# Splitting attention weights during the first MLP: one piece per call against four steps of a period each

## The chip, the core and the metric

The kernel runs on one core of one Trainium2 chip. The metric is the device time of one execution in microseconds (us); a profile of one execution is read beside it. Engines are named as in the profile: PE does the matrix products, PEld loads their weights, DVE, ACT and POOL do elementwise work, and SP issues the DMA transfers. PEclk is the clock granted to PE as a share of full speed.

## The reference, cut to what matters

One sequence of 512 tokens with 1024 channels passes a pooling mixer, an MLP, a stick-breaking attention and another MLP, all in f32.

```python
def sq_relu_mlp(h, w_up, w_down):          # 1024 -> 4096 -> 1024
    u = jnp.matmul(h, w_up)
    return jnp.matmul(jnp.square(jax.nn.relu(u)), w_down)

for layer in range(DEPTH):                 # DEPTH = 2
    h = rms_norm(x, mix_pre_g[layer])
    if layer < N_A:
        m = pool_mixer(h, pool_w[layer], pool_scale[layer])
    else:
        q = jnp.matmul(h, w_q[j])...       # 16 heads of 64
        o = stick_breaking_attention(q, k, v)
        m = jnp.matmul(o..., w_o[j])
    x = x + rms_norm(m, mix_post_g[layer])
    h = rms_norm(x, mlp_pre_g[layer])
    x = x + rms_norm(sq_relu_mlp(h, w_up[layer], w_down[layer]), mlp_post_g[layer])
    if layer == N_A - 1:
        kv = jnp.matmul(rms_norm(x, kv_norm_g), w_kv)...
```

## The kernel before

*Split numbers.* PE multiplies in a type with fewer digits than f32 (fp32r in the profile). So each f32 operand is split into hi (a cast, on ACT) and lo (operand minus hi, on DVE), and a product is three matmuls (`mm3`): hi by hi, hi by lo, lo by hi. `split` does this for activations and MLP operands (lines 233 and 234), `weight` for a weight matrix: load (L117), scaling by a gain on POOL where it has one (L139, in two halves), cast (L127), subtraction (L129).

*MLP.* Each MLP has 32 up blocks (`up_block`, 24 matmuls, lines 599 to 601) followed by relu and square on ACT. The down product is taken group by group: the class `Seven` multiplies 2 x 2 blocks with seven products in place of eight (`product`, L499), for groups of 2, 3, 3, 3 and 3 blocks, 35 products in all. `left` and `right` make the operands a and w of a product by sums and differences (POOL L454, DVE L473) and a split. A group's down weights come in two halves (L438): the first into the tile w1, the second into xn3 (shown as `xn`). The last four up blocks go with four plain down matrices ("dn"), which `contract` multiplies at the end of the MLP (lines 254 to 256); these matrices take over tiles that the groups no longer need.

*Attention weights ahead of time.* The attention needs 8 v, 8 q and 8 k matrices, scaled by gains, and 8 o matrices; each is 128 x 1024, 512 KB. While the first MLP runs, `split_apart` is called after each of its products (twice after two of them). A call takes the next matrix (a piece) off the list `apart`, loads it (L181), scales it if it has a gain, casts it (L184) and subtracts (L185), in this one call; two calls later a call stores both halves to DRAM (`kept`, L171). Pieces alternate between two sets of tiles: apart0 with apart1, and the work tiles spare with grow. In the attention, `make` loads the halves back with two transfers (L193) into a weight tile.

*Tiles.* Up weights, and in the attention its weights, take the next of four tiles with the tag "w" in the pool wts (`place`). What a tile holds next is loaded when its last reader is done.

*Order.* The program names what each engine does; a scheduler that simulates the engines sets the order of instructions on each engine, except inside `manual_schedule`, where PE keeps the order of the program. Each engine then runs in that order and waits where an operand or a tile is late.

## Time and profile before

| | us |
|---|---|
| median of 3 runs | 1009.63 |
| lowest and highest | 1008.39, 1012.03 |
| profiled execution, its own time | 1010.19 |
| span of the profiled execution | 1008.4 |

| engine | busy us | share of the span |
|---|---|---|
| PE | 957.0 | 95% |
| PEld | 812.1 | 81% |
| DVE | 744.5 | 74% |
| ACT | 521.7 | 52% |
| POOL | 248.6 | 25% |

The granted clock was 0.977 of full speed in the mean. Times in the rows are counted from the start of the span. A row of the waits says which engine and line waited for which engine and line, how long in all, how many times, and the longest. A row of a timeline gives the start and the length, and in brackets the idle time just ahead of it with what ended it.

### The profile page before, as it was taken

Reading aid. Unit: us, or ns where it says so; the run is one execution under the profiler, and the core shown is the slowest. Engines: PE = TensorE matmul, PEld = TensorE weight load, DVE = VectorE, ACT = ScalarE, POOL = GpSimd, SP = SyncE. Lnnn points to the kernel's source line nnn. Section 1 sums busy time; section 2 is a strip of 40 time slices with the busy share of each in tenths; the row PEclk is TensorE's granted clock in tenths of the full one; section 3 lists DMA queues with packets and bytes.
Section 4 is the critical chain, followed back from the end, with each engine's and each line's share of the span. In section 5 each row is a group of like instructions: output and inputs, shape, how many; then the busy total and the mean of one; then the engine's idle time right before and its main releaser. Section 6 shows DMA issues by size and latency. Waiting matters only on the chain.

```text
span 1008.4 us, 12461 instructions
## 1 busy us (share of the span) xinstructions
PE 957.0 (95%) x4823; PEld 812.1 (81%) x4823; DVE 744.5 (74%) x771; ACT 521.7 (52%) x837; POOL 248.6 (25%) x166
## 2 busy tenths in 40 slices
PE   7899889899799999899999999989999999999996
PEld 6897667678588788799888899879888888888885
DVE  5988598698797883747647778886488685967856
ACT  5656555445455452655565555566554444444532
POOL 1656262283350210500000000242031120402103
PEclk9999989989899999999999999999999999999998
DMA  7277957958869632042542425233333315133002
GB/s 264 72 286 269 317 204 280 317 196 279 305 233 338 242 126 84 21 165 88 175 158 85 167 94 190 93 131 121 126 104 125 125 42 174 35 127 125 5 38 85
DMA packets 44844, 161.59 MB, mean 160 GB/s; under 512 B 4592, under 2 KB 4976, under 8 KB 44784
## 3 DMA queue, kind: packets, MB, share of 16 engines
q1 hardware_dynamic: 44784, 160.79, 45.3%
q8 instruction: 38, 0.62, 0.2%
q14 instruction: 22, 0.18, 0.1%
HBM read 125.12 MB, written 35.65 MB: 159 GB/s over the span
## 4 chain that ended last, share of the span: by engine, by line
PE 61%; DVE 14%; DMA 12%; POOL 5%; issue 4%; ACT 3%; SPq 0%; POOLq 0%; DVEq 0%; ACTq 0%
PE ps L499 17%; PE ps L599 10%; PE ps L601 10%; PE ps L600 10%; DMA kept<-apart 5%; PE ps L254 3%; PE ps L255 3%; PE ps L256 3%; PE ps L843 2%; DVE x L285 2%; PE ps L833 2%; POOL apart L139 2%; DVE w L129 2%; DMA apart<-in_wk 2%; DMA kept<-spare 1%
## 5 line engine op out<-in xcount | busy, mean ns | idle before, releaser
L499 PE MATMUL ps<-w,a 128*128 128x512 f32 x1176 | 287.7, 398 | 24.0 <-DVE w L234 12.1
L499 PEld LDWEIGHTS ps<-w,a 128*128 128x128 f32 x1176 | 224.9, 192 | 76.1 <-DVE w L234 14.7
L600 PE MATMUL ps<-xnl,w 128*128 128x512 f32 (+1 forms) x712 | 262.4, 369 | 1.1 <-DVE xnl L234 1.1
L601 PE MATMUL ps<-xnh,w 128*128 128x512 f32 (+1 forms) x712 | 262.2, 369 | 0.0
L599 PE MATMUL ps<-xnh,w 128*128 128x512 f32 (+1 forms) x712 | 261.4, 370 | 0.0
L600 PEld LDWEIGHTS ps<-xnl,w 128*128 128x128 f32 x712 | 134.8, 189 | 23.3 <-DVE xnl L234 1.3
L601 PEld LDWEIGHTS ps<-xnh,w 128*128 128x128 f32 x712 | 134.8, 189 | 22.5
L599 PEld LDWEIGHTS ps<-xnh,w 128*128 128x128 f32 x712 | 134.2, 189 | 22.1
L508 DVE TENSOR_TENSOR y<-ps,y 128x512 f32<-128x512 f32 x124 | 83.5, 683 | 45.9 <-PE ps L499 45.9
L129 DVE TENSOR_TENSOR w<-raw,w 128x1024 fp32r<-128x1024 f32 x62 | 83.8, 1355 | 36.7 <-ACT w L127 36.6
L279 POOL TENSOR_TENSOR y<-y,grow 128x512 f32<-128x512 f32 x12 | 17.9, 1493 | 319.6 <-ACT xn L237 319.6
L454 POOL TENSOR_TENSOR s<-r 128x768 f32<-128x768 f32 (+1 forms) x10 | 23.1, 2310 | 240.9 <-ACT r L530 240.9
L233 ACT CAST a<-r 128x768 fp32r<-128x768 f32 (+1 forms) x60 | 47.5, 793 | 59.0 <-PE ps L499 25.4
L233 ACT CAST w<-e 128x1536 fp32r<-128x1536 f32 (+1 forms) x30 | 41.9, 1395 | 57.8 <-DVE e L473 51.8
L127 ACT CAST w<-raw 128x1024 fp32r<-128x1024 f32 x66 | 68.7, 1042 | 3.4 <-DMA raw<-in_wup 3.0
L234 DVE TENSOR_TENSOR a<-r,a 128x768 fp32r<-128x768 f32 (+1 forms) x60 | 67.0, 1118 | 4.1 <-ACT a L233 4.0
L529 ACT ACTIVATE r<-ps 128x512 f32<-128x512 f32 x56 | 33.2, 593 | 67.4 <-PE ps L601 67.3
L454 POOL TENSOR_TENSOR r<-r 128x768 f32<-128x768 f32 (+1 forms) x20 | 53.1, 2653 | 45.0 <-DVE a L234 44.3
L234 DVE TENSOR_TENSOR w<-e,w 128x1536 fp32r<-128x1536 f32 (+1 forms) x30 | 55.8, 1860 | 4.0 <-ACT w L233 3.7
L815 DVE TENSOR_TENSOR_SCAN e<-u,begin 128x1280 f32<-128x1280 f32 x16 | 45.1, 2820 | 13.2 <-ACT u L809 13.0
L139 POOL TENSOR_TENSOR spare<-spare,gc 128x512 f32<-128x512 f32 x24 | 36.3, 1531 | 66.0 <-DMA spare<-in_wq 37.4
L139 POOL TENSOR_TENSOR apart<-apart,gc 128x512 f32<-128x512 f32 x24 | 39.2, 1652 | 33.2 <-DMA apart<-in_wk 20.5
(134 smaller groups left out, 1595.6 us busy)
## 6 DMA issues: line engine op xcount, KB each, us to landing
raw<-in_wup SPq DMA_DIRECT2D x64, 512.0 KB, 4.0
w<-kept SPq DMA_DIRECT2D x62, 512.0 KB, 4.1
kept<-apart SPq DMA_DIRECT2D x48, 512.0 KB, 4.2
w<-in_wdn SPq DMA_DIRECT2D x8, 1536.0 KB, 7.9
xn<-in_wdn SPq DMA_DIRECT2D x8, 1536.0 KB, 7.1
kept<-spare SPq DMA_DIRECT2D x16, 512.0 KB, 5.4
spare<-in_wq SPq DMA_DIRECT2D x8, 512.0 KB, 4.1
apart<-in_wk SPq DMA_DIRECT2D x8, 512.0 KB, 4.8
```

What stands on the lines that cost most here:

```text
L127: nc.scalar.copy(hi, raw)
L129: on.tensor_tensor(out=lo, in0=raw, in1=hi.bitcast(F32), op=ALU.subtract)
L139: nc.gpsimd.tensor_tensor(out=v[:, h], in0=v[:, h], in1=g[:, h].broadcast_to((P, n // 2, D // n)), op=ALU.mult)
L233: latest["act"] = nc.scalar.copy(hi, src)
L234: latest["dve"] = nc.vector.tensor_tensor(out=lo, in0=src, in1=hi.bitcast(F32), op=ALU.subtract)
L454: sub = lambda out, x, y, op=ALU.subtract: nc.gpsimd.tensor_tensor(out=out, in0=x, in1=y, op=op)
L499: nc.tensor.matmul(bank, a[:, x, q, TS[t]], w[:, z, q], start=start and q == 0 and k == 0, stop=q == self.n - 1 and k == 2, skip_group_che ...
L508: nc.vector.tensor_tensor(out=part, in0=bank, in1=part, op=ALU.add)
L599: nc.tensor.matmul(pu[:, cols], wh[:, k, :], xnh[:, k, cols], start=k == 0, stop=False)
L600: nc.tensor.matmul(pu[:, cols], wh[:, k, :], xnl[:, k, cols], start=False, stop=False)
L601: nc.tensor.matmul(pu[:, cols], wl[:, k, :], xnh[:, k, cols], start=False, stop=k == KC - 1)
L815: nc.vector.tensor_tensor_scan(out=e[:, ::-1], data0=u[:, 1:][:, ::-1], data1=begin[:, ::-1], initial=0.0, op0=ALU.mult, op1=ALU.max,)
```

## The change

`split_apart` now moves each piece by one step per call: load in the first call, scaling in the next, cast and subtraction in the third, store in the fourth. There is one call after each product. Raw pieces rotate over four tiles (grow, spare and two tiles "apart"). The hi halves alternate between the two halves of one tile "wx". This tile is taken from the up weights: the tag "w" has three tiles now, and in the attention every fourth weight goes to "wx". Only v, q and k go this way (24 pieces); the o matrices are split in the attention by `weight`. Of the four plain down matrices of an MLP, the third now takes the two tiles "apart" and the fourth a tile "w". `contract` of the MLP is put under `manual_schedule` for PE.

```diff
--- before.py
+++ after.py
@@ -156,34 +156,42 @@
         elif k == ("o", 7):
             return [att_pool[0].tile([P, NSEG], F32R, tag="w", bufs=2, name=name(x))[:, :D] for x in "hl"]
         else:
-            both = wts.tile([P, 2, D], F32R, tag="w", bufs=4, name=name("w"))
+            count[0] += 1
+            fourth = count[0] % 4 == 0 and att_pool[0] is not None
+            both = wts.tile([P, 2, D], F32R, tag="wx" if fourth else "w", bufs=1 if fourth else 3, name=name("w"))
         return [both[:, 0], both[:, 1]]
     apart, kept, going = [], {}, []
     def split_apart(mp):
-        if len(going) > 1 or not apart and going:
-            k, parts = going.pop(0)
+        if going and going[0] is not None and going[0][1] == 3:
+            k, _, raw, hi, _ = going.pop(0)
             kept[k] = dram.tile([2, P, D], F32, tag=f"kept{len(kept)}", name=name("kept"))
-            for n in range(2):
-                nc.sync.dma_start(kept[k][n], parts[n].bitcast(F32))
-        if not apart:
-            return
-        k, src, scaled = apart.pop(0)
-        if len(apart) % 2:
-            raw = mp.tile([P, D], F32, tag="apart0", name=name("apart"))
-            hi = mp.tile([P, D], F32R, tag="apart1", name=name("apart"))
-        else:
-            raw = spare_tile()
-            hi = work.tile([P, D], F32R, tag="grow", name=name("apart"))
-        nc.sync.dma_start(raw, src)
-        if scaled is not None:
-            scaled(raw)
-        nc.scalar.copy(hi, raw)
-        nc.vector.tensor_tensor(out=raw, in0=raw, in1=hi.bitcast(F32), op=ALU.subtract)
-        going.append((k, (hi, raw)))
+            for n, t in enumerate((hi.bitcast(F32), raw)):
+                nc.sync.dma_start(kept[k][n], t)
+        if apart:
+            k, src, scaled = apart.pop(0)
+            n = len(apart) % 4
+            if n < 2:
+                raw = mp.tile([P, D], F32, tag="apart", bufs=2, name=name("apart"))
+            else:
+                raw = spare_tile() if n == 2 else work.tile([P, D], F32, tag="grow", name=name("apart"))
+            nc.sync.dma_start(raw, src)
+            going.append([k, 0, raw, None, scaled])
+        for x in going:
+            k, n, raw, hi, scaled = x
+            if n == 1:
+                scaled(raw)
+            elif n == 2:
+                hi = x[3] = apart_hi[0][:, len(kept) % 2]
+                nc.scalar.copy(hi, raw)
+                nc.vector.tensor_tensor(out=raw, in0=raw, in1=hi.bitcast(F32), op=ALU.subtract)
+            x[1] += 1
+    count, apart_hi = [0], [None]
     def make():
         k, src, scaled = queue.pop(0)
@@ -220,7 +228,7 @@
                 elif what == "O" and 0 in part or what == "E":
                     for c in range(2 * i, 2 * i + (2 if what == "O" else 4)):
                         want(("o", c), wo[c])
-            apart.extend(queue[n:])
+            apart.extend(x for x in queue[n:] if x[0][0] != "o")
             queue[n - GRP : n + GRP] = queue[n : n + GRP] + queue[n - GRP : n]
         for j in range(NJ):
@@ -541,6 +549,8 @@
         groups[0].load(0)
         groups[0].squares()
+        if l == 0:
+            apart_hi[0] = wts.tile([P, 2, D], F32R, tag="wx", name=name("wx"))
         need(0, 1)
         n0 = 2 * GROUPS[0]
         first = [(ps(), get(("up", l, j))) for j in range(n0)]
@@ -564,8 +574,7 @@
             for i in range(7):
                 group.product(i, y, written if g == 0 else None)
                 if l == 0:
-                    for _ in range(2 if i == 3 and g in (1, 2) else 1):
-                        split_apart(mp)
+                    split_apart(mp)
                 if i + 2 < 7:
                     if ups:
                         up(ups.pop(0))
@@ -581,16 +590,16 @@
                         coming.make(i + 2 - 7)
                     elif i == 5:
                         piece = lambda tag, k, bufs=1: mp.tile([P, k, D], F32R, tag=tag, bufs=bufs, name=name("dn"))
-                        w, e, x, z = piece("w1", 3), piece("e", 1), piece("w", 3, 2), piece("w", 3, 2)
-                        dn_pool[0] = [
-                            [w[:, 0], w[:, 1]], [w[:, 2], e[:, 0]], [x[:, 0], x[:, 1]], [x[:, 2], z[:, 0]],
-                        ]
+                        w, e, x = piece("w1", 3), piece("e", 1), piece("w", 3, 2)
+                        c, d = (piece("apart", 1, 2)[:, 0] for _ in range(2))
+                        dn_pool[0] = [[w[:, 0], w[:, 1]], [w[:, 2], e[:, 0]], [c, d], [x[:, 0], x[:, 1]]]
         assert not apart and not going
         gpost = gain_row((R_MLP_POST0, R_MLP_POST1)[l])
         w = [get(("dn", l, j)) for j in range(plain, NJ)]
         dn_pool[0] = None
         fill(ahead)
-        contract(squares[1:], w, y, False, lambda t, y: update(t, y, gpost))
+        with tc.manual_schedule(engines={mybir.EngineType.PE}):
+            contract(squares[1:], w, y, False, lambda t, y: update(t, y, gpost))
     def up_block(pu, w, cols):
         wh = w[0].rearrange("p (k c) -> p k c", k=KC)
```

Line numbers move by up to 9: casts of pieces stand at L190, splits of operands at L241, up blocks at L608 to L610.

First place: ACT in the first MLP, at the operands of the second group's first product (a of 128x768). Pieces are `apart` and `spare`. Before:

```order
L233 CAST a_1115<-r_497 128x512
L233 CAST w_1118<-xn_80 128x1024
L184 CAST apart_1174<-apart_1173 128x1024
L184 CAST apart_1358<-spare_1357 128x1024
L529 ACTIVATE r_774<-ps_1083 128x512
L127 CAST w_1110<-raw_1111 128x1024
L530 ACTIVATE r_774<-r_774 128x512
L233 CAST a_1149<-r_774 128x768
L233 CAST w_1153<-w_995 128x1536
```

Now:

```order
L241 CAST a_1102<-r_497 128x512
L241 CAST w_1105<-xn_80 128x1024
L127 CAST w_972<-raw_973 128x1024
L190 CAST wx_498<-apart_1410 128x1024
L537 ACTIVATE r_775<-ps_1070 128x512
L538 ACTIVATE r_775<-r_775 128x512
L127 CAST w_1036<-raw_1037 128x1024
L241 CAST a_1135<-r_775 128x768
L241 CAST w_1139<-w_984 128x1536
```

Two casts of pieces stood between the operand cast into w and the next relu (L529); now there is one, behind the cast of an up matrix, and it reads a piece loaded two calls earlier.

Second place: POOL at the end of the mixer, where the norm of the last tokens is made (`stat_440` and `m_439`). Before:

```order
L250 TENSOR_TENSOR stat_356<-stat_356,mhalf 128x1
L250 TENSOR_TENSOR stat_440<-stat_440,mhalf 128x1
L294 TENSOR_TENSOR m_439<-x_73,spare_129 128x512
L250 TENSOR_TENSOR stat_440<-stat_440,mhalf 128x1
L139 TENSOR_TENSOR spare_885<-spare_885,gc 128x512 x2
L139 TENSOR_TENSOR apart_823<-apart_823,gc 128x512 x2
```

Now:

```order
L258 TENSOR_TENSOR stat_356<-stat_356,mhalf 128x1
L258 TENSOR_TENSOR stat_440<-stat_440,mhalf 128x1
L139 TENSOR_TENSOR apart_824<-apart_824,gc 128x512
L302 TENSOR_TENSOR m_439<-x_73,spare_129 128x512
L139 TENSOR_TENSOR apart_824<-apart_824,gc 128x512
L258 TENSOR_TENSOR stat_440<-stat_440,mhalf 128x1
L139 TENSOR_TENSOR spare_881<-spare_881,gc 128x512 x2
```

The first piece's scaling (L139) followed the norm; now its halves stand ahead of `m_439` and ahead of the last power.

Third place: PE at the start of the attention, at the end of the k block of the first head pair (into `ps_3245` before, `ps_3162` now) and the beginning of its q block (`ps_3360`, `ps_3277`). w_2785 and w_2701 are k's weights, w_2849 and w_2762 are q's, w_2651 and w_2578 v's. Before:

```order
L256 MATMUL ps_3284<-w_2721,xnl 128x256
L599 MATMUL ps_3245<-xnh,w_2785 128x256
L599 MATMUL ps_3360<-xnh,w_2849 128x512
L254 MATMUL ps_3394<-w_2651,xnh 128x256
L255 MATMUL ps_3394<-w_2651,xnh 128x256
L600 MATMUL ps_3245<-xnl,w_2785 128x256
L601 MATMUL ps_3245<-xnh,w_2785 128x256
L599 MATMUL ps_3245<-xnh,w_2785 128x256
```

Now:

```order
L610 MATMUL ps_3162<-xnh,w_2701 128x256
L608 MATMUL ps_3162<-xnh,w_2701 128x256
L609 MATMUL ps_3162<-xnl,w_2701 128x256
L610 MATMUL ps_3162<-xnh,w_2701 128x256
L608 MATMUL ps_3277<-xnh,w_2762 128x512
L609 MATMUL ps_3277<-xnl,w_2762 128x512
L262 MATMUL ps_3311<-w_2578,xnh 128x256
L263 MATMUL ps_3311<-w_2578,xnh 128x256
```

The k and q blocks began together, from two tiles "w". Now q's block begins right after k's last matmul, and w_2762 is given the tile that w_2701 had. On SP its load stands behind those of the plain down weights and of k:

```order
L201 DMA w_2578<-kept_1000 128x1024 x2
L201 DMA w_2640<-kept_1061 128x1024 x2
L117 DMA raw_2854<-in_wdn 128x1024
L117 DMA raw_2858<-in_wdn 128x1024
L201 DMA w_2701<-kept_1125 128x1024 x2
L117 DMA raw_3878<-in_wo 128x1024
L117 DMA raw_3916<-in_wo 128x1024
L107 DMA grow_3069<-in_grow 128x1024
L201 DMA w_2762<-kept_1156 128x1024 x2
L201 DMA w_3274<-kept_1198 128x1024 x2
L201 DMA w_3382<-kept_1337 128x1024 x2
```

In SP's order of the first MLP, from the second piece's load (`spare_881`) to the load of the second weight half of the third group, stand 19 loads of pieces, 36 stores of halves, 14 up matrices (0.524 MB each) and 8.4 MB of down weights, 44.6 MB together; to that of the second group it is 25.7 MB.

## The prediction

> **What bounds the kernel now.** I cut the span into stages first, because the share of busy time is a mean over all of them. Columns: stretch, its length, busy time and count for PE, weight load, DVE, ACT and POOL, then granted clock, DMA share and GB/s.
>
> ```profile
> core 0: us, PE busy (x) PEld busy (x) DVE busy (x) ACT busy (x) POOL busy (x), PEclk, DMA share, GB/s
> 0.00:53.72 53.72, 43.49 (x315) 39.65 (x316) 41.70 (x78) 32.70 (x73) 22.59 (x24) 0.94 0.48 165
> 53.72:74.48 20.76, 20.76 (x152) 19.81 (x153) 16.53 (x17) 12.91 (x18) 10.02 (x7) 1.00 0.86 325
> 74.48:396.08 321.60, 297.62 (x1257) 241.49 (x1255) 258.06 (x208) 163.94 (x194) 119.83 (x63) 0.95 0.70 248
> ...
> 415.00:671.00 256.00, 254.47 (x1521) 226.36 (x1522) 179.48 (x225) 147.33 (x325) 26.53 (x37) 0.99 0.37 130
> ...
> 696.98:981.45 284.47, 284.47 (x1256) 235.63 (x1256) 202.16 (x176) 136.24 (x163) 51.04 (x20) 1.00 0.29 95
> 981.45:1008.41 26.96, 17.60 (x89) 14.86 (x88) 18.01 (x30) 5.69 (x18) 9.15 (x8) 0.89 0.22 79
> ```
>
> The two MLPs run the same matmuls (1257 and 1256 of them). The second takes 284.47 us and PE never stops; the first takes 321.60, which is 37.1 more. Of this 321.60 - 297.62 = 24.0 is idle PE, and 297.62 - 284.47 = 13.15 is the slower clock (0.95). So each idle microsecond costs another 13.15 / 24.0 = 0.55, and I multiply PE stalls by 1.55. Only the first MLP prepares attention weights. The waits of PE from 50 to 420 us (total, times, longest) say what it waits for:
>
> ```profile
> PE ps L499 <- DVE w L234: 12.1, 4, 5.3
> PE ps L499 <- ACT w L233: 9.4, 2, 7.6
> PE ps L326 <- ACT xn L317: 3.9, 1, 3.9
> PE ps L499 <- DVE a L234: 2.4, 3, 1.0
> ```
>
> 12.1 + 9.4 + 2.4 = 23.9, which is the idle time of the stage: it is the MLP's own operands that come late, though the products are equally large in the second MLP. I followed the longest, 7.6 us before 129.67, back through the timelines of four engines (start, length, idle before and its releaser in brackets):
>
> ```profile
> 116.24 0.39 PE L601 MATMUL ps<-xnh,w 128*128 128x512 f32 x1
> 116.47 5.60 PE L499 MATMUL ps<-w,a 128*128 128x512 f32 x24
> 129.67 1.22 PE L499 MATMUL ps<-w,a 128*128 128x512 f32 x2 [7.60 <-ACT w L233]
> ...
> 120.06 1.05 ACT L184 CAST apart<-apart 128x1024 fp32r<-128x1024 f32 x1 [4.48 <-POOL apart L139]
> 124.52 1.04 ACT L184 CAST apart<-spare 128x1024 fp32r<-128x1024 f32 x1 [3.41 <-POOL spare L139]
> ...
> 128.15 1.47 ACT L233 CAST w<-w 128x1536 fp32r<-128x1536 f32 x1
> ...
> 117.04 2.98 POOL L139 TENSOR_TENSOR apart<-apart,gc 128x512 f32<-128x512 f32 x2 [9.39 <-DVE a L234]
> 122.45 2.04 POOL L139 TENSOR_TENSOR spare<-spare,gc 128x512 f32<-128x512 f32 x2 [2.42 <-DVE apart L185]
> ...
> 118.25 0.33 SPq L181 DMA_DIRECT2D spare<-in_wq  x1
> ```
>
> Read it backwards. PE waits for ACT's w of 128.15. ACT had stood 4.48 and 3.41 us at the casts of two attention pieces (L184), which wait for POOL to scale them (L139), and POOL started the second only when its load, issued at 118.25, was there. ACT runs in order, so relu, squares and operand casts queue up behind a piece whose data is under way. It is the rule, not one accident:
>
> ```profile
> ACT apart L184 <- POOL spare L139: 40.0, 10, 6.9
> ACT apart L184 <- POOL apart L139: 35.5, 12, 6.1
> ```
>
> 75 us of waiting in 22 casts. Most is absorbed by slack on PE's side; 24 us is not.
>
> **The change, part by part.**
>
> *Four steps a period apart: -37.1, and what stays.* A piece is loaded in one period and scaled, cast and subtracted, and stored in the next three. A period is 284.47 / 35 products = 8.1 us. In the order of ACT around that place, two casts of pieces stood back to back ahead of the relu; now one stands there, and SP issues the load about two pieces ahead. ACT's 4 us waits then have 8 to 16 us of cover, and no row of the first MLP has another cause of comparable size. Ends: all of 37.1 goes, or none. I take all, and charge separately what can come instead. The three waits for a (2.4 us in the list above) are the MLP's own order: 2.4 x 1.55 = 3.7 stays (0 to 3.7).
>
> *The stream.* Loads that go out early need bytes early. In SP's order, from the second piece's load up to the third group's second weight half, stand 44.6 MB (19 piece loads, 36 half stores and 14 up matrices of 0.524 MB each, 8.4 MB of down weights), and 25.7 MB up to the second group's. What rate does the chip give?
>
> ```profile
> 696.98:813.98 117.00, 117.00 (x517) 96.91 (x517) 83.71 (x72) 59.64 (x75) 25.69 (x11) 1.00 0.34 114
> 50.00:190.00 140.00, 128.75 (x623) 107.69 (x622) 111.29 (x95) 78.82 (x104) 63.71 (x37) 0.96 0.77 274
> 114.00:131.00 17.00, 9.40 (x39) 7.51 (x38) 10.76 (x13) 8.70 (x12) 8.34 (x6) 0.83 0.95 355
> ```
>
> The first MLP moved 274 GB/s over 140 us, 355 in the stretch where SP had a backlog (DMA share 0.95), and 325 in the stage from 53.72 to 74.48 above. The first row gives the due time: from the first product to the third group's second, which is the first to need that half, PE takes 117.0 us (517 matmuls of 0.226). The same way the second group's half is due after 246 matmuls, 55.7 us. If the first product starts at 74.48 + 5 = 79.5 (the 5 is worked out below), combining and splitting the half want 4 us, and the stretch of loads begins at 54.3 with the end of the mixer, then 44.6 MB have 79.5 + 117.0 - 4 - 54.3 = 138.2 us, which is 323 GB/s, and 25.7 MB have 76.9 us, 334 GB/s. At 355 both are in time. At 325 the first is 79.1 - 76.9 = 2.2 late and the second not later. At 274 the second is 44.6 MB in 162.7 us, 24.5 late. In before's 274, SP stood waiting for tiles, so it is what was asked for, not what was to be had; I take 325, the row of the same mix just ahead: 2.2 x 1.55 = 3.4 (0 to 38).
>
> *Fewer slots for up weights: 0.* Three tiles instead of four: a slot comes round every 3 x 8.1 = 24.4 us, its matmuls take 24 x 0.226 = 5.4, so 19 stay for cast and subtraction, 1.04 + 1.36 = 2.4 by these groups (busy, mean ns):
>
> ```profile
> L127 ACT CAST w<-raw 128x1024 fp32r<-128x1024 f32 x66 | 68.7, 1042 | 3.4 <-DMA raw<-in_wup 3.0
> L129 DVE TENSOR_TENSOR w<-raw,w 128x1024 fp32r<-128x1024 f32 x62 | 83.8, 1355 | 36.7 <-ACT w L127 36.6
> ```
>
> If the 19 were gone it would be 2.4 at each of 28 blocks; nothing suggests that.
>
> *The start: +5.* POOL's order puts the first piece's scaling, in two halves, into the last tokens' norm, one ahead of its m and one ahead of its last pow.
>
> ```profile
> 52.39 0.55 POOL L250 TENSOR_TENSOR stat<-stat,mhalf 128x1 f32<-128x1 f32 x1 [0.82 <-DVE stat L243]
> 55.79 2.04 POOL L139 TENSOR_TENSOR spare<-spare,gc 128x512 f32<-128x512 f32 x2 [2.86 <-DMA spare<-in_wv]
> ...
> 54.98 0.28 PE L599 MATMUL ps<-xnh,w 128*128 128x256 f32 x1
> 55.10 0.28 PE L600 MATMUL ps<-xnl,w 128*128 128x256 f32 x1
> ```
>
> Both halves take 2.04, and every norm step behind them feeds PE's transposes. The same piece made POOL wait 2.86 for its load here. Ends: 0 (the halves fit in POOL's gaps) to 2.04 + 2.86 = 4.9; I take 2.04, since the load goes out earlier now. The fourth up block's first half used to fill PE there; its slot is now the first block's, which is in use: 24 matmuls at 0.12 (54.98 to 55.10) = 2.9 come out of the cover (0 to 2.9). Together 5 (0 to 8).
>
> *Attention: q0, +6.4, and o, +1.* q0's tile now is k0's. So SP can load it only after k0's last matmul, and PE's next two rows are q0's. The time from issue to landing of such a load is known:
>
> ```profile
> L193 SPq DMA_DIRECT2D w<-kept x62: 319/392/543, 346.9 to 625.6; - x62
> ...
> DMA to landing us min/median/max: 3.1/4.1/8.0
> ```
>
> Behind that load SP has the next v and k pieces (w_3274, w_3382), and behind q0's first matmul PE has the v products of w_2578, which is long there and could have run. PE stands 4.1 (median; 3.1 to 8.0) and, with the clock, 4.1 x 1.55 = 6.4 (4.8 to 12.4; with only a shorter wait, because PE's rows run ahead of it, 3.1). The Trainium skill, "TensorE: Matmul & The Clock Gate", Part 1, "What's actually happening", says that the clock falls to half after about 3.4 us idle and comes back after about 3.4 us of work. By that rule this wait would add 1.7 us in place of 2.3, and the sum would be 0.6 lower. The trace speaks for more rather than less: after the wait of 3.88 us here (timeline of PE, then its stretch)
>
> ```profile
> 201.07 2.50 PE L499 MATMUL ps<-w,a 128*128 128x512 f32 x5 [3.88 <-DVE w L234]
> ...
> 195.00:208.00 13.00, 9.12 (x28) 6.94 (x27) 12.10 (x11) 5.45 (x6) 5.88 (x3) 0.74 0.67 234
> ```
>
> 28 matmuls took 9.12 us, where 28 x 0.226 = 6.3 would do (117.00 / 517 from the row of the second MLP above). So 2.8 were lost behind one wait of 3.88, more than the mean of 0.55 per microsecond gives (2.1); I keep the mean. The eight o pieces are split in attention again: 8 x 1.04 on ACT, 8 x 1.36 = 10.8 on DVE, which is busy for 179.48 of 256.00 there. Ends 0 and 8 x 2.40 = 19.2; I take 1, for the 76 us of slack.
>
> *Last down weights and the fixed order: -2 and -1.5.* The fourth plain matrix no longer needs the last product's tiles, so its split is ready earlier and the first token tile's sums end first, in both MLPs.
>
> ```profile
> 414.89 1.73 PE L326 MATMUL ps<-ident,xn 128*128 128x128 f32 x8 [3.92 <-ACT xn L317]
> ...
> 998.77 0.28 PE L256 MATMUL ps<-dn,sq 128*128 128x256 f32 x1
> ...
> 999.79 1.40 DVE L285 SCALAR_TENSOR_TENSOR x<-y,stat,x 128x512 f32<-128x512 f32 x2
> 1001.12 0.41 DVE L361 TENSOR_TENSOR y<-ps,y 128x256 f32<-128x256 f32 x1
> ```
>
> The handoff wait is 3.92 in the first (0 to -3.9; I take half). At the end, the last sums leave PE at 998.77 + 0.28 and DVE fetches them at 1001.12, behind the updates of x at 999.79: 2.07 between (0 to -2.07), of which I take 1.5, as one update of two is passed.
>
> Sum: -37.1 + 3.7 + 3.4 + 5 + 6.4 + 1 - 2 - 1.5 = -21.1. The profiled execution took 1010.19 us (span 1008.4): 989.1. Its time is 0.56 above the median of the three runs (1009.63), so 988.5 for the median.
>
> **Rivals.**
>
> *The stream stays at 274 GB/s: slower.* For it: before shows it over 140 us, with stores of the same size among the loads. Against: SP waited for tiles while it did, and 355 was granted when it had work. Place: the second half of the second and third groups' down weights, PE waiting for DVE's or ACT's w behind the load. Price 24.5 x 1.55 = 38 instead of 3.4: 988.5 + 34.6 = 1023. It decides where the lateness is (21.1 + 3.4) / 1.55 = 15.8 us, at 44.6 MB in 138.2 + 15.8 us = 290 GB/s; at less the change loses.
>
> *The wait moves to the two halves of the new hi tile.* The cast of a piece needs the store of the piece two before it to have landed. If SP is behind by more than two periods, ACT stands at the cast as now. For: SP's queue is in order, and stores stand behind loads that wait for tiles. Against: 16 us of cover. At half the old idle time: 12 x 1.55 = 18.6 in place of 3.7: 1003. This gives faster, by little.
>
> *Everything fits.* The start costs nothing, the stream 355: 988.5 - 5 - 7.1 = 976.
>
> *The change doesn't do what it says.* Then ACT's order would be as it was; the rows show otherwise. What is left is that gains and prices meet: within 3 us of before.
>
> **How the numbers follow.** About 0.3%, 3 us, is what a measurement of this kernel can tell from no change. Forecast, 982 to 996: 0.48 (stream of 311 to 345 GB/s). Everything fits, below 982: 0.15. The half gain, 996 to 1006.6: 0.17. Within 3 us: 0.08. Slower: 0.12, the slow stream. So faster 0.48 + 0.15 + 0.17 = 0.80. The range 974 to 1010 leaves out some 0.03 below and 0.15 above.
>
> **What would show it.** Right: the first MLP's stage at about 292 us with PE's waits for w under 6 us; ACT's waits for POOL at casts of pieces from 75 us to under 15; DMA above 310 GB/s in the first half of the stage; one PE wait of about 4 us for a DMA at q0. Wrong: PE waits for w released by transfers of down weights, ACT waiting for the hi tile's stores, or more than 8 us between the last mixer matmuls and the first product.

## The result, and the profile after

The changed kernel takes 999.92 us (median of 4, 998.85 to 1002.42) against 1010.83 (4 runs) for the kernel before on the same chip: ratio 0.9895, 95% interval 0.9862 to 0.9928. It is 1.05% faster where 2.1% was forecast; 988.5 us was predicted. The profiled execution took 1002.42 us, 2.5 above the median, so the stages below give a little less gain than the medians.

The stages of the changed kernel (columns as ahead of the prediction), from the last transposes of the mixer on:

```profile
55.96:78.90 22.94, 22.70 (x153) 21.27 (x153) 17.89 (x16) 13.17 (x18) 11.20 (x7) 0.93 1.00 378
78.90:382.44 303.54, 291.59 (x1256) 237.96 (x1255) 252.75 (x201) 158.81 (x187) 125.43 (x60) 0.98 0.59 216
382.44:401.91 19.47, 19.47 (x96) 16.31 (x96) 14.84 (x26) 13.67 (x34) 9.23 (x10) 1.00 0.00 1
401.91:691.66 289.75, 277.44 (x1665) 245.68 (x1664) 200.16 (x245) 164.61 (x345) 24.43 (x37) 0.99 0.32 110
691.66:993.89 302.23, 302.23 (x1345) 250.66 (x1343) 217.88 (x199) 141.47 (x179) 55.33 (x27) 1.00 0.29 95
993.89:1000.60 6.71, 0.00 (x0) 0.00 (x0) 2.98 (x8) 0.63 (x4) 0.88 (x2) 0.66 0.34 121
```

Cut at the same marks (first product, last product, last plain matmul, first product of the second MLP, last matmul), the two profiled executions compare as follows, with the prediction's terms beside:

| stage, us | before | after | change | forecast |
|---|---|---|---|---|
| start to the first product | 74.48 | 78.90 | +4.4 | +5 |
| products of the first MLP | 321.76 | 303.54 | -18.2 | -30.0 |
| plain down matrices, first MLP | 24.23 | 19.47 | -4.8 | -2 |
| attention | 276.35 | 289.75 | +13.4 | +7.4 |
| second MLP | 302.23 | 302.23 | 0 | 0 |
| tail | 9.35 | 6.71 | -2.6 | -1.5 |
| span | 1008.40 | 1000.60 | -7.8 | -21.1 |

Two rows carry the miss: the products (11.8 us less gain than forecast) and the attention (6.0 more loss). The miss would be larger without the plain matrices and the tail, which gave 3.9 more than forecast. PE's longest waits in the products and the attention (total, times, longest):

```profile
PE ps L507 <- ACT w L241: 5.4, 2, 3.7
PE ps L608 <- DMA w<-kept: 3.4, 1, 3.4
PE ps L507 <- DVE w L242: 3.1, 2, 2.7
PE ps L507 <- DVE a L242: 2.5, 2, 1.5
```

And ACT's waits at the casts of pieces, from 55 to 405 us:

```profile
ACT wx L190 <- POOL apart L139: 27.4, 12, 5.4
ACT wx L190 <- POOL spare L139: 8.2, 5, 2.9
```

The long stall of 7.6 us is gone, and ACT's waits at pieces fell from 75.5 to 35.6 us. But 12 us of idle PE are left in the products, in seven stalls from 89 to 222 us. The longest, 3.69 us before 142.11, is followed back here over PE, ACT, DVE and POOL:

```profile
142.11 0.73 PE L507 MATMUL ps<-w,a 128*128 128x512 f32 x2 [3.69 <-ACT w L241]
...
140.58 1.47 ACT L241 CAST w<-e 128x1536 fp32r<-128x1536 f32 x1 [4.78 <-DVE e L481]
...
130.15 2.59 DVE L242 TENSOR_TENSOR w<-w,w 128x1536 fp32r<-128x1536 f32 x1
132.66 2.86 DVE L191 TENSOR_TENSOR apart<-apart,wx 128x1024 f32<-128x1024 f32 x1
135.44 2.60 DVE L242 TENSOR_TENSOR a<-r,a 128x768 fp32r<-128x768 f32 x1
137.96 2.59 DVE L481 TENSOR_TENSOR e<-xn,w 128x1536 f32<-128x1536 f32 x1
...
127.38 3.74 POOL L139 TENSOR_TENSOR apart<-apart,gc 128x512 f32<-128x512 f32 x2
131.09 3.35 POOL L462 TENSOR_TENSOR r<-r 128x768 f32<-128x768 f32 x1
134.52 2.70 POOL L462 TENSOR_TENSOR r<-s,r 128x768 f32<-128x768 f32 x1
137.18 4.27 POOL L139 TENSOR_TENSOR apart<-apart,gc 128x512 f32<-128x512 f32 x2
```

ACT's w waits for DVE's e, and DVE has no gap ahead of it: it works from 130 to 140 us without a pause. What is odd is the lengths. A subtraction of 128x1024 (L191) takes 2.86 us, one of 128x768 (L242) 2.60; the kernel before shows 1.22 for 128x1024 in the second MLP (below). POOL is busy throughout, and its scaling of two halves takes 3.74 and 4.27 where 2.04 was shown. So this stall isn't a piece that is late: instructions of both engines take longer here. Split in half, the stage says where:

```profile
78.90:225.00 146.10, 134.15 (x568) 107.81 (x567) 135.93 (x99) 82.59 (x102) 102.48 (x51) 0.98 0.81 303
225.00:382.44 157.44, 157.44 (x689) 130.14 (x689) 116.83 (x104) 76.21 (x86) 22.95 (x10) 0.99 0.39 137
```

All stalls lie in the first half, with DVE 93% and POOL 70% busy. The second half has none.

The two halves also hold a control. DVE's subtraction of an up matrix (L129) reads two work tiles, which the kernel has in SBUF. Its addition into y (L516) reads one of these and one tile `ps`, which the kernel has in PSUM and PE fills with its sums. The groups in the first half (busy us, mean ns of one, idle before), then in the second:

```profile
L129 DVE TENSOR_TENSOR w<-raw,w 128x1024 fp32r<-128x1024 f32 x15 | 26.8, 1788 | 3.1 <-ACT w L127 2.9
L516 DVE TENSOR_TENSOR y<-ps,y 128x512 f32<-128x512 f32 x24 | 16.0, 678 | 0.3 <-PE ps L507 0.3
```

```profile
L129 DVE TENSOR_TENSOR w<-raw,w 128x1024 fp32r<-128x1024 f32 x12 | 14.6, 1218 | 12.5 <-ACT w L127 12.5
L516 DVE TENSOR_TENSOR y<-ps,y 128x512 f32<-128x512 f32 x38 | 25.9, 685 | 17.7 <-PE ps L507 17.7
```

The subtraction takes 1788 ns in the half with a busy POOL and 1218 in the other; the addition takes the same in both. Taken one by one in this run from 50 us on, the 53 subtractions of this line that no POOL instruction overlaps took 1.20 to 1.23 us, and the 13 that POOL overlaps for over nine tenths 1.94 in the mean.

Of the signs that the prediction named for being right, only the wait at q0 came. The products are 303.5 us and not 292, PE's waits for w 8.5 and not under 6, ACT's waits at pieces 35.6 and not under 15, and the first half of the stage moved 303 GB/s and not over 310.

### The profile page after: what moved, and what is told of

It is laid out like the page before. It is cut to its first block, busy times and chain, and to the rows that moved or that the text cites. A ratio compares the mean times of both kernels' runs of the same rounds, so it can differ in the third digit from the quotient of the medians.

```text
span 1000.6 us, 12426 instructions
## 1 busy us (share of the span) xinstructions
PE 957.6 (96%) x4823; PEld 811.4 (81%) x4823; DVE 745.1 (74%) x771; ACT 525.0 (52%) x837; POOL 249.9 (25%) x166
## 4 chain that ended last, share of the span: by engine, by line
PE 74%; DVE 11%; issue 5%; DMA 3%; ACT 3%; POOL 3%; SPq 0%; POOLq 0%; DVEq 0%; ACTq 0%
PE ps L507 22%; PE ps L609 12%; PE ps L608 12%; PE ps L610 12%; PE ps L262 4%; PE ps L263 4%; PE ps L264 4%; DVE w L242 2%; PE ps L852 2%; DVE apart L191 1%; DVE a L242 1%; PE ps L842 1%; DVE w L129 1%; POOL apart L139 1%; DMA apart<-in_wk 1%
## 5 line engine op out<-in xcount | busy, mean ns | idle before, releaser
L507 PE MATMUL ps<-w,a 128*128 128x512 f32 x1176 | 282.1, 393 | 12.0 <-ACT w L241 5.4
L507 PEld LDWEIGHTS ps<-w,a 128*128 128x128 f32 x1176 | 222.0, 190 | 61.9 <-ACT w L241 6.2
L608 PE MATMUL ps<-xnh,w 128*128 128x512 f32 (+1 forms) x712 | 262.5, 371 | 3.7 <-DMA w<-kept 3.4
L610 PE MATMUL ps<-xnh,w 128*128 128x512 f32 (+1 forms) x712 | 262.1, 369 | 0.0
L608 PEld LDWEIGHTS ps<-xnh,w 128*128 128x128 f32 x712 | 134.9, 190 | 26.2 <-issue 3.6
L610 PEld LDWEIGHTS ps<-xnh,w 128*128 128x128 f32 x712 | 135.0, 190 | 22.3
L129 DVE TENSOR_TENSOR w<-raw,w 128x1024 fp32r<-128x1024 f32 x69 | 95.1, 1379 | 51.0 <-ACT w L127 50.8
L516 DVE TENSOR_TENSOR y<-ps,y 128x512 f32<-128x512 f32 x124 | 83.9, 684 | 49.8 <-PE ps L507 49.7
L127 ACT CAST w<-raw 128x1024 fp32r<-128x1024 f32 x73 | 76.3, 1046 | 50.3 <-PE ps L610 29.7
L241 ACT CAST a<-r 128x768 fp32r<-128x768 f32 (+1 forms) x60 | 47.7, 795 | 80.1 <-PE ps L507 40.6
L139 POOL TENSOR_TENSOR apart<-apart,gc 128x512 f32<-128x512 f32 x36 | 66.2, 1861 | 24.1 <-DMA apart<-in_wk 21.2
L242 DVE TENSOR_TENSOR w<-e,w 128x1536 fp32r<-128x1536 f32 (+1 forms) x30 | 68.5, 2284 | 4.9 <-ACT w L241 4.4
L242 DVE TENSOR_TENSOR a<-r,a 128x768 fp32r<-128x768 f32 (+1 forms) x60 | 66.9, 1117 | 4.5 <-ACT a L241 4.5
L241 ACT CAST w<-e 128x1536 fp32r<-128x1536 f32 (+1 forms) x30 | 41.9, 1397 | 53.1 <-DVE e L481 43.3
L462 POOL TENSOR_TENSOR r<-r 128x768 f32<-128x768 f32 (+1 forms) x20 | 44.9, 2246 | 41.4 <-DVE a L242 40.9
L242 DVE TENSOR_TENSOR w<-w,w 128x1536 fp32r<-128x1536 f32 (+1 forms) x20 | 34.6, 1729 | 4.2 <-ACT w L241 4.2
```

What stands on the lines that cost most here:

```text
L127: nc.scalar.copy(hi, raw)
L129: on.tensor_tensor(out=lo, in0=raw, in1=hi.bitcast(F32), op=ALU.subtract)
L139: nc.gpsimd.tensor_tensor(out=v[:, h], in0=v[:, h], in1=g[:, h].broadcast_to((P, n // 2, D // n)), op=ALU.mult)
L241: latest["act"] = nc.scalar.copy(hi, src)
L242: latest["dve"] = nc.vector.tensor_tensor(out=lo, in0=src, in1=hi.bitcast(F32), op=ALU.subtract)
L462: sub = lambda out, x, y, op=ALU.subtract: nc.gpsimd.tensor_tensor(out=out, in0=x, in1=y, op=op)
```

## The experiments

Times are medians; ratios are against the kernel before on the same chip, with 95% intervals; stages, in us, are from one profile each. The products of the changed kernel come out at 303.5, and at 303.9 (q0 in wx) and 300.5 (calls spread) where they hold the same work, so a difference of some 3 us in one stage tells nothing by itself.

| run | us | ratio | start | products | attention |
|---|---|---|---|---|---|
| changed kernel | 999.9 | 0.9895 (0.9862-0.9928) | 78.9 | 303.5 | 289.8 |
| no scaling | 985.1 | 0.9742 (0.9714-0.9770) | 77.8 | 287.1 | 288.5 |
| one store | 1016.6 | 1.0060 (1.0044-1.0075) | 77.0 | 318.8 | 290.7 |
| q0 in wx | 991.7 | 0.9811 (0.9783-0.9840) | 77.1 | 303.9 | 282.4 |
| o kept | 994.0 | 0.9829 (0.9802-0.9856) | 79.1 | 300.4 | 283.8 |
| before + last part | 1003.3 | 0.9949 (0.9931-0.9967) | 76.3 | 319.1 | 273.8 |
| q0 in wx, o kept | 988.5 | 0.9800 (0.9783-0.9818) | 78.2 | 301.4 | 279.3 |
| calls spread | 1000.1 | 0.9911 (0.9897-0.9926) | 78.5 | 300.5 | 289.7 |
| scaling on ACT | 989.4 | 0.9808 (0.9787-0.9828) | 80.6 | 287.9 | 289.2 |
| ACT, q0 in wx | 978.9 | 0.9697 (0.9672-0.9721) | 81.8 | 289.3 | 281.5 |
| ACT, q0, o kept | 979.3 | 0.9708 (0.9691-0.9724) | 79.8 | 287.8 | 281.6 |
| before, scaling on ACT | 991.6 | 0.9830 (0.9813-0.9846) | 77.3 | 300.6 | 275.6 |
| ACT, q0, held start | 981.4 | 0.9730 (0.9715-0.9744) | 77.0 | 292.2 | 281.5 |
| ACT + idle POOL work | 1006.7 | 0.9969 (0.9953-0.9985) | 82.7 | 302.5 | 289.9 |

**No scaling.**

```diff
             if n == 1:
-                scaled(raw)
+                pass
```

> The changed kernel with the scaling of the pieces on POOL left out (24 times two instructions of 1.0 us, or 1.7 to 3.5 where DVE works beside them); loads, casts, subtractions and stores stay, so the kept weights lack their gains. Theory 'POOL and DVE slow each other': the changed kernel's remaining stalls at 142, 207, 212 and 222 us (8.8 us) come from DVE and POOL instructions that run 1.5 to 2 times as long while the other runs; without the scaling the first MLP falls from 303.4 to about 290 us and the time by 10 to 14 us. Theory 'the stream': the loads and stores are late; nothing but the scaling changes, so the first MLP stays within 4 us of 303. In both the start gets 2 us shorter.

This kernel leaves out the gains of the pieces. The time is 985.1, and the products fall to 287.1, 2.4 us above the 284.6 of the second MLP in the kernel before between the same marks. One stall of 2.35 us is left. The first half with its DMA rate:

```profile
77.77:221.00 143.23, 140.88 (x622) 116.35 (x621) 126.98 (x109) 89.78 (x109) 28.60 (x10) 1.00 0.90 333
```

The same pieces are loaded and stored, at 333 GB/s over this stretch: the stream is not what held PE.

**One store.** (The diff is shortened.)

```diff
-            kept[k] = dram.tile(...)
-            for n, t in enumerate((hi.bitcast(F32), raw)):
-                nc.sync.dma_start(kept[k][n], t)
+            if kept:
+                kept[k] = next(iter(kept.values()))
+            else: ...   # as before
```

> The changed kernel with the stores of all pieces but the first left out (46 of 48, 24 MB); the attention loads the first piece in place of each. Theory 'the stream': the waits for transfers (POOL for pieces 21 us, ACT for up weights 10.6) go, and the first MLP falls from 303.4 to 293 us or less. Theory 'POOL and DVE slow each other': the first MLP loses only the 1.7 us stall at 128.6, which stood behind an up weight's transfer, with its clock some 3 us.

Neither: it got slower, 1016.6, with products of 318.8. The stretch from the first product on:

```profile
76.99:135.00 58.01, 44.87 (x173) 35.78 (x172) 53.53 (x33) 33.15 (x44) 51.71 (x31) 0.85 0.59 190
```

And from its groups (busy us, mean ns of one) DVE's subtractions of up matrices:

```profile
L129 DVE TENSOR_TENSOR w<-raw,w 128x1024 fp32r<-128x1024 f32 x6 | 12.3, 2057 | 0.0
```

The pieces ran ahead: by 135 us 36 halves were scaled or in work, 24 in the changed kernel. POOL was 89% and DVE 92% busy, and PE stood for 13 of 58 us. The subtraction of an up matrix took 2057 ns there, against this group of the kernel before in its second MLP, where POOL does little:

```profile
L129 DVE TENSOR_TENSOR w<-raw,w 128x1024 fp32r<-128x1024 f32 x24 | 29.3, 1222 | 33.2 <-ACT w L127 33.0
```

So the stores had been holding the pieces back. Less transfer made it slower, which speaks against the stream a second time; and the longer subtractions go with 190 GB/s here, where the changed kernel's first half moved 303. There is a second route to the loss, though. PE's longest wait here, 8.73 us before 94.08, was for ACT's a, which waited for a combining on POOL (L465, from 91.14) that stood behind two halves of scaling (from 87.18).

**Scaling on ACT.**

```diff
+            if on is nc.scalar:
+                for b in range(n):
+                    nc.scalar.mul(v[:, b], v[:, b], gc[:, lo + b : lo + b + 1])
+                return
...
-                scaled(raw)
+                scaled(raw, nc.scalar)
```

> The changed kernel with the pieces scaled on ACT in place of POOL (one instruction for each gain, 8 for k and q, 4 for v). Theory 'POOL and DVE slow each other': DVE's instructions get back to the lengths of the run without scaling, and if ACT (160 of 303 us busy) takes the extra work, the products fall to 288 to 292 us. Rival: ACT runs in order, 2 to 3 us more of pieces stand ahead of relu and operand casts at each product, and the products stay at 300 or more.

989.4, products 287.9, as if the scaling were left out:

```profile
80.64:225.00 144.36, 141.65 (x622) 116.60 (x623) 128.22 (x108) 127.88 (x238) 30.48 (x12) 1.00 0.90 333
```

ACT is busy 127.9 of 144 us, and PE stands for 2.7 us in all of the products; DVE fell from 252.75 us of work in the products to about 233. This run and the one without scaling take away two things, though: POOL's work beside DVE, and ACT's waits for POOL. Hence the next.

**Scaling on ACT, and idle POOL work.**

```diff
                 scaled(raw, nc.scalar)
+                one = mp.tile([P, 1], F32, tag="one", bufs=2, ...)
+                nc.scalar.copy(one, raw[:, :1])
+                for _ in range(2):
+                    nc.gpsimd.tensor_tensor(out=idle[0], in0=idle[0], in1=one.broadcast_to(...), op=ALU.add)
```

> The kernel with the scaling on ACT, and beside it as much work on POOL as the scaling was, which nothing waits for: for each piece, after its scaling, one copy of a column on ACT and two additions of 128x512 into a tile of their own on POOL. If POOL slows DVE by working beside it, DVE's instructions get long again (128x1024 from 1.3 towards 1.6 us) and the products go from 288 back to 297 us or more. If what cost time was that ACT waited for POOL's scaled pieces, the products stay at 288 to 291. In between, at 291 to 297, both count.

1006.7, products 302.5, PE idle for 11.7 us in them: the loss is back, though nobody waits for this work. The first half, the group of the pieces' subtractions, and PE's waits in the products:

```profile
79.00:225.00 146.00, 135.34 (x572) 108.67 (x571) 137.72 (x97) 123.76 (x251) 101.17 (x52) 0.98 0.87 320
```

```profile
L204 DVE TENSOR_TENSOR apart<-apart,wx 128x1024 f32<-128x1024 f32 x15 | 25.4, 1695 | 2.5 <-ACT wx L203 2.5
```

```profile
PE ps L520 <- DVE w L255: 7.5, 6, 2.0
PE ps L520 <- ACT a L254: 3.2, 2, 1.9
PE ps L520 <- DVE a L255: 1.0, 2, 0.5
```

DVE is at 137.7 of 146 us again, and the pieces' subtraction at 1695 ns (1326 with the scaling on ACT, 1617 in the changed kernel). So POOL's work costs by running beside DVE. 7.5 of the 11.7 us are waits for w, which only DVE and ACT make. The rest, for a, may in part be POOL's own combinings, which now queue behind the idle work: ACT's waits for them rose from 9.9 to 11.7 us.

**Calls spread.**

```diff
-                if l == 0:
+                n = 7 * g + i
+                if l == 0 and (n + 1) * 27 // 35 > n * 27 // 35:
                     split_apart(mp)
```

> The changed kernel with the 27 calls spread evenly over the 35 products (no call after every fourth or fifth product). Theory 'too dense': in the first half of the first MLP DVE is 93% busy and POOL 70%, since each slows the other; spread out, both have slack everywhere and the products fall from 303.5 to 293 us or less. Rival 'single meetings': a stall arises wherever a scaling meets the combining of a group's first operands, dense or not; the products stay within 4 us of 303, with stalls now in the second half too.

1000.1, which decides nothing, since the work was not spread:

```profile
78.45:225.00 146.55, 135.96 (x577) 109.69 (x576) 138.38 (x99) 83.22 (x102) 102.17 (x52) 0.98 0.82 303
```

POOL is 102 us busy in the first half, as without this edit: the scheduler, which sets the order on each engine, has the pieces as early as before, wherever the calls stand. Whether pieces spread over the whole MLP would stall less stays open.

**Before, scaling on ACT.** The kernel before with the ACT loop above, everything else as it was.

> The kernel before (load, scale, cast and subtraction in one call) with the scaling on ACT in place of POOL. Theory 'POOL and DVE slow each other' as the whole cause: the products fall from 322 to 300 us or less without the four steps. Theory of the prediction, that ACT stands at a piece whose load has just been issued: ACT now waits for the transfers themselves, its order is as bad as it was, and the products stay at 315 or more; the steps are then needed as well.

991.6, products 300.6. That is at the first theory's end: 21 us go without the four steps, by taking the work from POOL alone. With the steps as well the products fall by another 12.7, to 287.9, so both count. How the 21 us divide isn't shown. ACT no longer waits for POOL at the pieces, where it waited 75.5 us in the kernel before, but for their loads (22.6 us) and others. Its largest waits at pieces from 50 to 400 us are these (the profile shows no releaser for "issue"):

```profile
ACT apart L188 <- issue: 20.0, 4, 6.1
ACT spare L139 <- DMA spare<-in_wq: 7.8, 4, 3.9
ACT apart L139 <- DMA apart<-in_wk: 7.1, 3, 4.9
```

In all, its waits at pieces fall from 95.2 to 55.9 us. And the casts of pieces don't stand back to back in this kernel's ACT order. So part of the 21 us may be shorter waits and order, and not POOL beside DVE; a kernel before with idle POOL work would tell, and was not run.

**q0's tile.**

```diff
+            if k == ("q", 0):
+                count[0] = 0
-            fourth = count[0] % 4 == 0 and att_pool[0] is not None
+            fourth = count[0] % 4 == 0 and (att_pool[0] is not None or k == ("q", 0))
```

> The changed kernel with q0's weights put into the tile wx, which is free then, in place of k0's. If q0's load behind k0's last matmul costs what the profile shows (3.42 us of wait, 1.15 at the first scores, and the clock at 0.83 over the next 10 us, 1.7 to 2), the time falls by 5 to 7 us. If the next loads or the tile order in the attention make up for it, it stays within 2.

991.7; the attention fell by 7.4, from 289.8 to 282.4. What it cost stands in PE's timeline of the changed kernel, and in the stretch of ten microseconds behind:

```profile
421.95 0.47 PE L608 MATMUL ps<-xnh,w 128*128 128x512 f32 x1 [3.42 <-DMA w<-kept]
```

```profile
422.00:432.00 10.00, 10.00 (x48) 8.85 (x48) 0.39 (x1) 0.17 (x1) 0.00 (x0) 0.83 0.36 127
```

**o kept.** (The diff is shortened: a piece without a gain, as o's are, also skips the scaling.)

```diff
-            apart.extend(x for x in queue[n:] if x[0][0] != "o")
+            apart.extend(queue[n:])
```

> The changed kernel with the eight o pieces split in the first MLP as well, 32 pieces in the same four steps (o has no gain to scale). If o's split in the attention costs DVE time where DVE is full (612 to 632 us, clock 0.83), the attention gets 5 to 8 us shorter, and the second half of the first MLP, which has no stall now, stays as it is: 4 to 8 us faster. Rival: eight more pieces bring 8 x (0.5 + 1.0) MB and 2.4 us of ACT and DVE each, the first MLP takes as much longer, and the time stays within 3 us.

994.0; the attention fell by 6.0 and the products did not grow (300.4). The place is late in the attention of the changed kernel, where DVE has no gap:

```profile
612.00:622.00 10.00, 8.05 (x48) 6.28 (x46) 10.00 (x12) 4.74 (x8) 0.00 (x0) 1.00 0.35 105
622.00:632.00 10.00, 9.27 (x34) 7.17 (x35) 9.43 (x15) 4.73 (x9) 0.00 (x0) 0.83 0.51 138
```

> The changed kernel with q0 in the tile wx and the eight o pieces kept, both edits of the runs before together. If they are apart from each other, 8.2 and 5.9 us add up: 986 us, attention at 276 as in the kernel before. If both repair the same queueing at the start of the attention or take turns at the tiles, 989 or more.

Both together: 988.5, between the two numbers, with the attention at 279.3 in place of 276. PE has a longer wait there, 3.4 us for the split of xn in place of 0.5, so the two don't quite add up.

**The last part alone**, in the kernel before (the diff is shortened):

```diff
-                        w, e, x, z = piece("w1", 3), piece("e", 1), piece("w", 3, 2), piece("w", 3, 2)
...
+                        c, d = piece("apart0", 1)[:, 0], piece("apart1", 1)[:, 0]
+                        dn_pool[0] = [[w[:, 0], w[:, 1]], [w[:, 2], e[:, 0]], [c, d], [x[:, 0], x[:, 1]]]
...
+        with tc.manual_schedule(engines={mybir.EngineType.PE}):
```

> The kernel before with the last part of the change alone: the third plain down matrix in the tiles apart0 and apart1, the fourth in a tile w, and contract of the MLP in a fixed PE order. In the changed kernel the stretch from the last product to the last plain matmul fell from 24.2 to 19.5 us and the tail from 9.35 to 6.7. If these come from this part alone, the time falls by 7 us and the products stay at 322. If they need the other parts (earlier ends of the splits), by less than 4.

Ratio 0.9949 (0.9931 to 0.9967), some 5 us, between the two forecasts. The plain stage fell to 19.47 and the tail to 6.80, as in the changed kernel, so these 7.3 us of the profile are this part's. Its two halves, the tiles and the fixed order, were not taken apart.

**Putting it together.** Scaling on ACT and q0 in wx; then o kept as well; then (over the first of these) the pieces held behind the last norm:

> The changed kernel with the scaling on ACT and q0 in the tile wx. The two gains lie in different stages (products 303.5 to 288, attention 289.8 to 282) and should add up: 989.4 - 8.2 = 981 us. If the loads of the attention come later because ACT ends its pieces later, 985 or more.

> The same with the eight o pieces kept too. With q0 moved, keeping o brought 3.2 us more (988.5 against 991.7): 978 us, if the products still have no stall. Rival: ACT is 89% busy in the first half with 24 pieces; with 32 in 35 calls the products get longer and the time is 981 or more.

> The kernel with the scaling on ACT and q0 in the tile wx, and with the pieces' scaling (ACT) and subtraction (DVE) held behind the split of the last tokens' normed activations. The first product starts at 81.8 us there, 74.5 in the kernel before. If pieces among the norm steps cost the start, it falls to 77 or less and the time to 974 to 976 us. If the first product is late because of the loads (pieces and stores beside the first down weights) or the missing fourth tile for up weights, the start stays above 80 and the time within 2 us of 979.

```diff
+                norm3.update(latest)            # behind need(2, 3)
...
+                with tc.issue_after(norm3["act"].ins):
                     scaled(raw, nc.scalar)
...
+                with tc.issue_after(norm3["dve"].ins):
                     nc.vector.tensor_tensor(out=raw, in0=raw, in1=hi.bitcast(F32), op=ALU.subtract)
```

The first takes 978.9 us, 3.0% less than the kernel before (ratio 0.9697, 0.9672 to 0.9721) and the fastest here. Keeping o adds nothing to it (979.3): the attention is 281.6 with and 281.5 without, and the wait of 3.4 us for the split of xn is there again. Holding the pieces shortens the start and gives it back later. PE at the last transposes without the hold:

```profile
56.48 1.06 PE L340 MATMUL ps<-ident,xn 128*128 128x128 f32 x8 [3.34 <-DVE xn L333]
```

With the hold, there and at a new stall in the second group:

```profile
53.06 1.06 PE L342 MATMUL ps<-ident,xn 128*128 128x128 f32 x8 [0.77 <-DVE xn L335]
...
138.92 1.65 PE L515 MATMUL ps<-w,a 128*128 128x512 f32 x3 [4.42 <-ACT a L249]
```

The wait for the norm falls from 3.34 to 0.77 and the first product starts at 77.0 in place of 81.8. But the second group has a new stall: ACT casts and scales pieces from 134.76 to 138.06, ahead of the cast of a that PE waits for, after it had waited 3.98 us for DVE's e, and DVE in turn 2.68 for a half of the down weights. The products are 2.9 us longer, and the time is not better (981.4).

## Why the prediction was right or wrong

*Four steps: the direction right, the step "no row of the first MLP has another cause of comparable size" wrong.* The queue of ACT behind unready pieces was there, and the steps took much of it away (75.5 us of waits to 35.6, products 18.2 us shorter). But PE's idle time had a second cause of comparable size, POOL's scaling beside DVE: in the changed kernel it costs the products some 15 us (302.5 with idle POOL work, 287.9 without). The whole 37.1 us was credited to the first; 18.2 came. The rows for the second were quoted in the prediction and not read: two halves of scaling took 2.98 us at 117.04 and 2.04 at 122.45, in one kernel with one shape. A length that differs for the same instruction is a finding, and I used the lower one as the price.

The Trainium skill, "GPSIMD Engine Reference", section 1 "Specifications", says that POOL's memory interfaces are shared with VectorE, with contention for VectorE instructions with two inputs from SBUF. The trace agrees: 2057 ns beside POOL and 1222 without, and DVE's additions with one input from PSUM took 678 and 685 ns, beside a busy POOL and without.

The change also put more of POOL's work into the same stretch, since pieces no longer hold each other up. POOL's scaling from 78 to 225 us, in the kernel before and then in the changed one:

```profile
L139 POOL TENSOR_TENSOR apart<-apart,gc 128x512 f32<-128x512 f32 x14 | 23.2, 1675 | 25.6 <-DMA apart<-in_wk 16.3 <-DVE a L234 9.4
L139 POOL TENSOR_TENSOR spare<-spare,gc 128x512 f32<-128x512 f32 x14 | 22.7, 1644 | 36.5 <-DMA spare<-in_wq 22.2 <-DMA spare<-in_wv 11.9 <-DVE apart L185 2.4
```

```profile
L139 POOL TENSOR_TENSOR apart<-apart,gc 128x512 f32<-128x512 f32 x29 | 55.4, 1936 | 15.4 <-DMA apart<-in_wk 15.4
L139 POOL TENSOR_TENSOR spare<-spare,gc 128x512 f32<-128x512 f32 x10 | 19.3, 1946 | 10.6 <-DVE y L516 6.0 <-DVE apart L191 4.5
```

There are 39 halves where there were 28, and one takes 1.9 us where it took 1.66: 74.7 us of scaling on POOL in place of 45.9. The 3.7 us that the prediction kept for three waits for a, as the MLP's own order, were not that either: without the scaling, PE's only stall of the products is one of 2.35 us for w.

*The stream: 3.4 us forecast, some 2.6 found; the slow rival refuted.* One stall of 1.66 us stood behind an up matrix's transfer, 2.6 with the prediction's factor for the clock. The rate was not a limit: 378 GB/s between the mixer and the first product, and 333 over half a stage when nothing else was in the way. The lateness that the rival priced at 38 us did not come.

*The wait at the two halves of the hi tile:* refuted as a cause; ACT's waits at the casts were for POOL (35.6 us), and without the scaling the same tile did, with 2.5 us of waits for its stores. This rival's time, 1003 us, lies near the measured one by chance.

*Attention: the q0 step right (6.4 forecast, 7.4 shown), the o step wrong (1 forecast, 6.0 shown).* I set 10.8 us of DVE work against 76 us of slack in 256 us of attention. The slack of a stage is not the slack at the place: DVE was 97% busy from 612 to 632 us, where five of the eight pieces were split. As for the clock behind q0's wait, the ten microseconds after it ran at 0.83, which is 1.7 lost; the mean of 0.55 per microsecond (1.9) is a little high. The Trainium skill's rule on the clock gate ("TensorE: Matmul & The Clock Gate", Part 1) fits here, with the 1.7 us that the prediction worked out from it; the 2.8 lost behind the wait of 3.88, in the prediction's rows, is more than that.

*Start: +4.4 for +5 in this pair of profiles, some +3 over several.* The stage was 74.5 and 76.3 us in the two kernels with the old start (before, last part alone) and 77.1 to 79.1 in five with the new one. The order did what was forecast, in the changed kernel:

```profile
51.40 1.04 POOL L139 TENSOR_TENSOR apart<-apart,gc 128x512 f32<-128x512 f32 x1 [2.92 <-DMA raw<-in_wup]
52.40 1.27 POOL L302 TENSOR_TENSOR m<-x,spare 128x512 f32<-128x512 f32 x1
53.62 1.03 POOL L139 TENSOR_TENSOR apart<-apart,gc 128x512 f32<-128x512 f32 x1
54.62 0.55 POOL L258 TENSOR_TENSOR stat<-stat,mhalf 128x1 f32<-128x1 f32 x1
```

POOL stood 2.92 us ahead of the piece, whose load landed at 51.26 (the releaser in the row is inferred, and names another transfer). The prediction put this wait at 0. So m began at 52.40 (49.82 in the kernel before). But POOL's scaling isn't needed for the loss: left out, it gave 77.8, with the piece's cast on ACT ahead of the norm's squares (1.48 us of wait for its load). With the pieces held behind the norm (in the kernel with ACT's scaling) 2.6 us of PE's wait went. So pieces among the norm steps cost the start; how much is each engine's is open.

*Up weights in three tiles: right (0);* without POOL's scaling the products come within 2.4 us of the second MLP's, with the three tiles. *Last part: right in sign, half in size* (-3.5 forecast, -7.4 in the profile): I took half of the handoff's wait of 3.92, and all of it went, with some 0.8 us more; at the tail 2.6 went where 1.5 was forecast.

## What to carry to other kernels

When one instruction of one shape shows two lengths in a trace, find out what ran beside it before pricing anything with it; two engines that slow each other can be the bound where neither is at 100%. Work that is "off the critical path" on POOL can cost PE time though nobody waits for it; a dummy of the same work, with no consumer, measures that. A second instruction of the slowed engine, with other operands, shows whether the engine or the operands' place is what matters. And set moved work against the slack at its place, in a window of some ten microseconds, not against that of its stage.

## What was not expected of the hardware

POOL work that nothing waited for cost 17.3 us (1006.7 against 989.4 us; some of it may be the column copies on ACT). Leaving out 24 MB of stores made the kernel 17 us slower (1016.6 against 999.9). And the transfers ran at 378 GB/s over 23 us with a DMA share of 1.00, where 355 was the most that the prediction had found.
